# The last layer's S5 parameters in smaller pieces, over the merge and the output projection

## The chip, the cores and the metric

The kernel runs on one core of one Trainium2 chip. The core has five engines with a queue of instructions each: TensorE (PE in the profile, its weight loads PEld), VectorE (DVE), ScalarE (ACT), GpSimd (POOL) and SyncE (SP). Here SP starts most transfers, POOL starts the stores of the S5 parameters. The metric is the device time of one execution in microseconds (us).

## The reference

Two layers work on 512 latent and 256 context tokens of width 1024. In each layer an input projection feeds three branches (differential attention, RG-LRU, S5), each branch is gated and projected, the three are merged by sigmoid gates, and an output projection is added to the stream:

```python
def gated_merge(ya, yr, ys, za, zr, zs, gl, w_branch, w_out):
    y = jnp.stack([ya * jax.nn.silu(za), yr * jax.nn.silu(zr), ys * jax.nn.silu(zs)], axis=2)
    yb = jnp.einsum('btnw,nwd->btnd', y, w_branch)
    g = jax.nn.sigmoid(gl.reshape(*gl.shape[:2], N_BRANCH, D_MODEL))
    return jnp.sum(g * yb, axis=2) @ w_out
```

The S5 branch is a complex diagonal state space. Its coefficients depend on parameters alone:

```python
    mag = jnp.exp(lr * dt)
    ar = mag * jnp.cos(li * dt)
    ai = mag * jnp.sin(li * dt)
    ...
    br = cr[..., None] * b_re - ci[..., None] * b_im
    bi = cr[..., None] * b_im + ci[..., None] * b_re
```

So whatever the kernel derives from them for the second layer (powers of a, tables, products with B and C) can be computed at any time before that layer's scan.

## The kernel before

Weights are float32. `wsplit` (L159 to L161) loads a block `wr`, ACT rounds it to `wh`, DVE subtracts to get `wl`; the activations are split likewise (`hH`, `hL`). `product` (L174) sums three matmuls per block: `wh` with the high and low halves, `wl` with the high half. A product over 768 tokens with 8 blocks is 48 matmuls (a 512 and a 256 wide one each time).

The end of layer 0 goes like this. `merge_y` (four times) makes the gated attention output `yH`, `yL` from an input projection. `merge_g(0, ...)` then runs eight steps `dt`: a gate product `ps_in` (48 matmuls, two weight splits), a branch product `ps_b` (24, one split), `g` from both on DVE (L872) and its sum into `m` (L873, on POOL for the first two steps, on DVE after). Steps 0 to 5 are followed by an adaLN product (`ps_ada`, L130, then transposes `ps_adat`, L135, and a reduce `mods` on DVE, L137). Then the output projection takes eight products `acc` or `ps_w` from `mH`, `mL`, with a residual `xn` each (L1139); the last three do the context tokens first and their latent half in `second()`. The context norm (L196 to L209) reads the residuals.

Into this, layer 0 also puts the S5 parameters of layer 1, by a generator `prepare()` that is advanced with `prep(n)`: powers, then for each of 16 pairs `pa` (with coefficients and tables every fourth) `vv` (L453 to L455) and `wt` (L500 to L504) on DVE, a strip of small matmuls `ps_st5` (L467 to L472) copied by ACT to `strip`, and four transposes `ps_wt` (L511) copied by ACT to `ws`. All are stored to `s5d` and `s5td` in HBM by POOL and fetched by SP in layer 1. `PIECES` says how often the generator is advanced: in each of the four `merge_y`, in each step of `merge_g`, in each product of the output projection. With `(2, 2, 2, 2), (3,) * 8, (2,) * 8` the 22 pieces of before are used up in merge step 4.

The order on each engine is set by the tile layer's scheduler from the order of emission, the data, and the buffers that are free. Tables `tb`, `strip`, `wt` and `ws` have one buffer, `vv` and `Bb` two; strips, transposes, adaLN and norm share two PSUM buffers (`mis`).

Of the kernel before, what the change touches and what calls it, by code (L numbers as in the profile page):

```python
# [35 lines left out]
        [[0, 2], [1, 0], [2, 1], [1, 0], [0, 1, 1, 0], [0, 1, 1, 0, 3, 1, 1, 0]])  # L36
S5_BUFS = 3

PIECES = ((2, 2, 2, 2), (3,) * 8, (2,) * 8)
EARLY = {2: (1, 3, 4, 5, 6), 0: (1, 2, 3, 4, 5)}  # L40
LATE = 3
ADD_V = (2, 8)
# [9 lines left out]
def hybrid_kernel(ctx, tc, xT, cc, wmod, win, winv, wbr, wout, wglu, wlru, par, lqk, s5a, s5b, s5B, s5C, dsk, rope, outT):  # L52
# [311 lines left out]
    s5d = pD.tile([16, 128, R_N], F32, name="s5d")  # L364
    s5e = pD.tile([8, 128, 4, 128], F32, name="s5td")


    def s5_params(l, p, VV, E, store=None, storet=None):

# [3 lines left out]
        def cmul(eng, orr, oi, xr, xi, yr, yi, t1, t2):  # L373
            eng.tensor_mul(t1, xr, yr)
            eng.tensor_mul(t2, xi, yi)
            eng.tensor_sub(orr, t1, t2)
            eng.tensor_mul(t1, xr, yi)
            eng.tensor_mul(t2, xi, yr)
            eng.tensor_add(oi, t1, t2)

        def s5_powers():
            asc = [p.tile([128, 64, 9], F32, name=f"asc{c}", tag="vv", bufs=VV) for c in range(2)]
            V.memset(asc[0][:, :, 0:1], 1.0)
            V.memset(asc[1][:, :, 0:1], 0.0)
            V.tensor_copy(asc[0][:, :, 1:2], ar[:, l * 64:(l + 1) * 64].unsqueeze(2))
            V.tensor_copy(asc[1][:, :, 1:2], ai[:, l * 64:(l + 1) * 64].unsqueeze(2))
            ct = [p.tile([128, 64, 4], F32, name=f"ct{c}", tag="UW"[c]) for c in range(2)]
            for m in (1, 2, 4):
                sh = [128, 64, m]
                cmul(V, asc[0][:, :, m + 1:2 * m + 1], asc[1][:, :, m + 1:2 * m + 1], asc[0][:, :, 1:m + 1],  # L390
                     asc[1][:, :, 1:m + 1], asc[0][:, :, m:m + 1].to_broadcast(sh),
                     asc[1][:, :, m:m + 1].to_broadcast(sh), ct[0][:, :, :m], ct[1][:, :, :m])
            for c in range(2):
                w4 = pw[c].rearrange("p (r d g) n -> p r d g n", d=2, g=2)
                a4 = asc[c].rearrange("p (r d g) n -> p r d g n", d=2, g=2)
                for g2 in range(2):
                    V.memset(w4[:, :, 0, g2, 0:1], 0.0)
                    V.memset(w4[:, :, 1, g2, 9:10], 0.0)
                    V.tensor_copy(w4[:, :, 0, g2, 1:10], a4[:, :, 0, g2, :])
                    V.tensor_copy(w4[:, :, 1, g2, 8::-1], a4[:, :, 1, g2, :])  # L400

        def s5_coeffs(qt):

# [17 lines left out]
        def s5_tables(qt):  # L421

            tb = p.tile([128, 2, 8, NCH], F32, name="tb", tag="tb")
            tt = [p.tile([128, 2, 8, 24], F32, name=f"tt{c}", tag="UW"[c]) for c in range(2)]
            b0 = l * 32 + qt * 8
            V.memset(tb[:, 0, :, 0:1], 1.0)
            V.memset(tb[:, 1, :, 0:1], 0.0)
            V.tensor_copy(tb[:, 0, :, 1:2], f8r[:, b0:b0 + 8].unsqueeze(2))
            V.tensor_copy(tb[:, 1, :, 1:2], f8i[:, b0:b0 + 8].unsqueeze(2))
            m = 1  # L430
            while m < NCH - 1:
                c = min(m, 24, NCH - 1 - m)
                for e in range(2):
                    V.tensor_mul(tt[e][:, :, :, :c], tb[:, :, :, 1:1 + c],
                                 tb[:, e, :, m:m + 1].unsqueeze(1).to_broadcast([128, 2, 8, c]))
                V.tensor_sub(tb[:, 0, :, m + 1:m + 1 + c], tt[0][:, 0, :, :c], tt[1][:, 1, :, :c])
                V.tensor_add(tb[:, 1, :, m + 1:m + 1 + c], tt[0][:, 1, :, :c], tt[1][:, 0, :, :c])
                m += c
            tbs[qt] = tb
            if store is not None:  # L440
                for r in range(4):
                    G.dma_start(store[4 * qt + r, :, R_TB:].rearrange("p (e b j) -> p e b j", e=2, b=2),
                                tb[:, :, 2 * r:2 * r + 2, :])

        def s5_vv(pa):

            qt, pr = pa // 4, pa % 4
            qs, pq = slice(pr * 4, pr * 4 + 4), slice(pa * 4, pa * 4 + 4)
            xC = xCs[qt]
            vv = p.tile([128, 4, 10, 16], F32, name="vv", tag="vv", bufs=VV)  # L450
            vu = p.tile([128, 4, 10, 16], F32, name="vu", tag="wu")
            sh = [128, 4, 10, 16]
            E.tensor_mul(vv, xC[:, 0, qs].unsqueeze(2).to_broadcast(sh), pw[0][:, pq].unsqueeze(3).to_broadcast(sh))  # L453
            E.tensor_mul(vu, xC[:, 1, qs].unsqueeze(2).to_broadcast(sh), pw[1][:, pq].unsqueeze(3).to_broadcast(sh))
            E.tensor_sub(vv, vv, vu)  # L455
            vfs[pa] = vv.rearrange("p q n h -> p q (n h)")
            if store is not None:
                G.dma_start(store[pa, :, :R_WS].rearrange("p (q n) -> p q n", q=4), vfs[pa])
# [33 lines left out]
        def s5_wt(pa):  # L492
            qt, pr = pa // 4, pa % 4
            qs, pq = slice(pr * 4, pr * 4 + 4), slice(pa * 4, pa * 4 + 4)
            Bb = Bbs[qt]

            wt = p.tile([128, 4, 8, 16], F32, name="wt", tag="wt")
            wu = p.tile([128, 4, 8, 16], F32, name="wu", tag="wu")
            sh = [128, 4, 8, 16]
            E.tensor_mul(wt, Bb[:, 0, qs].unsqueeze(2).to_broadcast(sh),  # L500
                         pw[0][:, pq, 8:0:-1].unsqueeze(3).to_broadcast(sh))
            E.tensor_mul(wu, Bb[:, 1, qs].unsqueeze(2).to_broadcast(sh),
                         pw[1][:, pq, 8:0:-1].unsqueeze(3).to_broadcast(sh))
            E.tensor_add(wt, wt, wu)  # L504
            wts[pa] = wt

        def s5_ws(pa):
            wt = wts[pa]
            pwt = mis("ps_wt")
            for q in range(4):  # L510
                PE.transpose(pwt[:, q * 128:(q + 1) * 128], wt[:, q].rearrange("p s h -> p (s h)"), ident)  # L511
            ws = p.tile([128, 4, 128], F32, name="ws", tag="ws5")
            S.activation(ws.rearrange("p q n -> p (q n)"), pwt, AF.Copy)
            wss[pa] = ws
            if store is not None:
                G.dma_start(store[pa, :, R_WS:R_TB].rearrange("p (q n) -> p q n", q=4), ws)

        def prepare():

            s5_powers()  # L520
            yield
            for pa in range(16):
                if pa % 4 == 0:
                    s5_coeffs(pa // 4)
                    s5_tables(pa // 4)
                    yield
                s5_vv(pa)
                s5_wt(pa)
                yield
                s5_strip(pa)  # L530
                s5_ws(pa)

        return SimpleNamespace(powers=s5_powers, coeffs=s5_coeffs, tables=s5_tables, vv=s5_vv, strip=s5_strip,
# [3 lines left out]
    def s5_make(l):  # L537
# [7 lines left out]
        if l == 0:  # L545
            pr_ = s5_params(l, p5, S5_BUFS, V)
# [96 lines left out]
        def s5_inner(pa):  # L643
            if pa % 4 == 0:
                pr_.coeffs(pa // 4)
            pr_.vv(pa)
            pr_.strip(pa)

        def ahead():
            for st in sts:  # L650
                V.memset(st[:, :, :, 0:1], 0.0)
            if l > 0:
                for p in range(3):
                    fetch(p)
                return
            pr_.powers()
            s5_inner(0)
            done[0] = 1
            pr_.tables(0)

        def step(pa):
            if pa == 0:
                s5_input(0)
                s5_scan(0)
            if l == 0 and done[0] < 16:
                s5_inner(done[0])
                done[0] += 1
            if pa + 1 < 16:
                if pa % 4 == 3:
                    s5_input(pa // 4 + 1)  # L670
                    if l == 0:
                        pr_.tables(pa // 4 + 1)
                s5_scan(pa + 1)
            s5_out(pa)
            if l > 0:
                fetch(pa + 3)
# [5 lines left out]
    for l in range(L):  # L682
# [404 lines left out]
        if l == 0:  # L1087
            prst, pPr = pool("s5prep", 1, side="right")
            ast, pAd = pool("wmod2", 4, side="right")
            pieces = s5_params(1, pPr, 2, V, s5d, s5e).prepare()  # L1090

            def prep(n):
                for _ in range(n):
                    next(pieces, None)
# [6 lines left out]
        for i in range(4):  # L1101
            merge_y(ZA_T, oT, i, y0, 0.5)
            prep(PIECES[0][i])
        for dt in range(KT):
# [6 lines left out]
            elif dt in (1, 4):  # L1111
                adaln(1, 4 + dt // 4, pAd)
            prep(PIECES[1][dt])
        ast.close()
# [32 lines left out]
        for dt in range(KT):  # L1147
# [17 lines left out]
            residual(dt, po, sg)  # L1165
            prep(PIECES[2][dt])
        if need:
# [124 lines left out]
```

## Time and profile before

| | |
|---|---|
| median of 3 runs | 1634.73 us (1633.6 to 1636.02) |
| profiled execution | 1631.08 us, span 1629.3 us |
| TensorE matmul, weight load busy | 1503.6 us (92%), 1256.4 us (77%) |
| VectorE busy | 1170.3 us (72%) |
| ScalarE, POOL busy | 752.9 us (46%), 122.3 us (8%) |
| mean granted TensorE clock | 0.962 of full speed |

The profile is of one execution. Times on its axis are microseconds from the first instruction. A busy share is the time in which the engine has an instruction under way; starting a transfer and waiting are not counted as busy. The granted clock is the share of TensorE's full speed that it was allowed, 0.5 being 1.2 GHz and 1.0 being 2.4 GHz.

### The profile page before, as it was taken

How to read it: one execution, taken by the hardware profiler on the slowest of the kernel's cores; microseconds unless marked ns; L12 is line 12 of the kernel's file. 1: busy time of each engine (PE TensorE's matmuls, PEld its weight loads, DVE VectorE, ACT ScalarE, POOL GpSimd, SP SyncE). 2: the span in 40 equal slices, each digit the busy share in tenths (PEclk: the TensorE clock that was granted, in tenths of full speed). 3: DMA queues.
4: the chain of work that ended last, by engine and by line, in shares of the span. 5: the costliest groups of instructions: out<-in, count | busy, mean ns of one | idle time of the engine just before them, and what ended most of it. 6: DMA issues, size and time to landing. Idle time of an engine off the chain costs nothing. (4 is left out here: it accounts for less than half of the span.)

```text
span 1629.3 us, 24552 instructions
## 1 busy us (share of the span) xinstructions
PE 1503.6 (92%) x9096; PEld 1256.4 (77%) x9096; DVE 1170.3 (72%) x2463; ACT 752.9 (46%) x1300; POOL 122.3 (8%) x175
## 2 busy tenths in 40 slices
PE   4997569999999999996699999999899999999997
PEld 2776458888988888885577888777788888888877
DVE  7899999974457757759898445388877467488555
ACT  7674335542345434543233335576533355355433
POOL 1000000000000000001455000000000000000020
PEclk9999769999999999997799999999999999999999
DMA  8432112132211111113588550344445312212442
GB/s 286 154 103 64 52 50 67 53 109 78 59 58 39 46 52 46 46 33 128 185 261 281 184 179 33 122 143 140 119 149 145 103 59 69 62 59 65 140 168 94
DMA packets 103144, 174.43 MB, mean 107 GB/s; under 512 B 24432, under 2 KB 41456, under 8 KB 103024
## 3 DMA queue, kind: packets, MB, share of 16 engines
q1 hardware_dynamic: 97392, 158.17, 30.8%
q0 software_dynamic: 5632, 14.69, 2.8%
q8 instruction: 72, 1.18, 0.3%
q14 instruction: 48, 0.39, 0.1%
HBM read 145.02 MB, written 25.69 MB: 105 GB/s over the span
## 5 line engine op out<-in xcount | busy, mean ns | idle before, releaser
L160 ACT ACTIVATE wh<-wr 128x512 fp32r<-128x512 f32 x320 | 200.2, 630 | 403.4 <-PE ps_in L174 192.8
L174 PE MATMUL ps_in<-hH,wh 128*128 128x512 f32 x1248 | 375.3, 359 | 11.3 <-ACT m L828 4.8
L174 PE MATMUL ps_in<-hH,wl 128*128 128x512 f32 x1248 | 375.8, 358 | 8.8 <-DVE wl L161 8.8
L161 DVE TENSOR_TENSOR wl<-wr,wh 128x512 fp32r<-128x512 f32 x320 | 229.4, 720 | 208.4 <-ACT wh L160 162.1
L174 PE MATMUL ps_in<-hL,wh 128*128 128x512 f32 x1248 | 372.4, 357 | 0.0
L174 PEld LDWEIGHTS ps_in<-hH,wh 128*128 128x128 f32 x1248 | 205.9, 190 | 48.8 <-ACT m L828 5.6
L174 PEld LDWEIGHTS ps_in<-hH,wl 128*128 128x128 f32 x1248 | 207.1, 190 | 44.3 <-DVE wl L161 10.3
L174 PEld LDWEIGHTS ps_in<-hL,wh 128*128 128x128 f32 x1248 | 205.5, 190 | 31.6 <-issue 0.2
L873 POOL TENSOR_TENSOR m<-m,g 128x768 f32<-128x768 f32 (+1 forms) x16 | 28.2, 1764 | 1174.5 <-DVE g L872 749.3
L1038 ACT ACTIVATE p<-ps_s,mx 128x768 f32<-128x768 f32 (+1 forms) x80 | 65.2, 816 | 71.5 <-DVE mx L1037 67.6
L174 PE MATMUL ps_b<-yH,wh 128*128 128x512 f32 (+1 forms) x288 | 88.5, 358 | 1.8 <-ACT wh L160 1.8
L174 PE MATMUL ps_b<-yH,wl 128*128 128x512 f32 (+1 forms) x288 | 88.2, 358 | 0.2 <-DVE wl L161 0.2
L174 PE MATMUL ps_b<-yL,wh 128*128 128x512 f32 (+1 forms) x288 | 88.1, 358 | 0.0
L1036 DVE TENSOR_REDUCE mx<-ps_s 128x1 f32<-128x768 f32 (+1 forms) x80 | 67.6, 847 | 23.5 <-PE ps_s L1033 22.9
L174 PEld LDWEIGHTS ps_b<-yH,wh 128*128 128x128 f32 x288 | 47.9, 188 | 11.7 <-ACT wh L160 3.0
L174 PEld LDWEIGHTS ps_b<-yH,wl 128*128 128x128 f32 x288 | 47.7, 188 | 7.6 <-DVE wl L161 0.3
L174 PEld LDWEIGHTS ps_b<-yL,wh 128*128 128x128 f32 x288 | 47.6, 188 | 7.2
L174 PE MATMUL acc<-mH,wl 128*128 128x512 f32 (+1 forms) x160 | 49.0, 339 | 0.0
L511 PE MATMUL ps_wt<-ident,wt 128*128 128x128 f32 x128 | 24.0, 317 | 27.0 <-DVE wt L504 15.9
L174 PE MATMUL acc<-mH,wh 128*128 128x512 f32 (+1 forms) x160 | 48.7, 337 | 0.0
L174 PE MATMUL acc<-mL,wh 128*128 128x512 f32 (+1 forms) x160 | 48.7, 337 | 0.0
L1030 PE MATMUL ps_s<-ks,qs 128*128 128x256 f32 (+1 forms) x144 | 42.5, 367 | 3.3 <-ACT ks L1004 1.4
(349 smaller groups left out, 2843.1 us busy)
## 6 DMA issues: line engine op xcount, KB each, us to landing
wr<-in_win SPq DMA_DIRECT2D x208, 256.0 KB
wm<-in_wmod SPq DMA_DIRECT2D x48, 512.0 KB
wr<-in_wbr SPq DMA_DIRECT2D x48, 256.0 KB
sp<-s5d SPq DMA_DIRECT2D x16, 768.0 KB
wr<-in_wout SPq DMA_DIRECT2D x32, 256.0 KB
s5d<-vv POOLq DMA_DIRECT2D x16, 320.0 KB, 3.3
usd<-up SPq DMA_DIRECT2D x8, 512.0 KB
vt<-usd SPq DMA_DIRECT2D x64, 64.0 KB
```

What stands on the lines that cost most here:

```text
L160: S.activation(wh, raw, AF.Copy)
L161: V.tensor_sub(wl, raw, f32(wh))
L174: PE.matmul(out[:, c0:c0 + n], lhsT=(wl if ps == 2 else wh)[:, k, :], rhs=rhs(k0 + k, ps == 1)[:, t0:t0 + n], start=st, stop=en)
L511: PE.transpose(pwt[:, q * 128:(q + 1) * 128], wt[:, q].rearrange("p s h -> p (s h)"), ident)
L873: (V if n == 0 and dt >= ADD_V[l] else G).tensor_add(m_t[dt][:, :W], m_t[dt][:, :W], g[:, :W])
L1030: PE.matmul(sc[:, c0:c0 + w], lhsT=qs[:, c, qt * 128:(qt + 1) * 128], rhs=kk[:, c, t0:t0 + w], start=True, stop=False)
L1036: V.reduce_max(mx[:, 0:1], sc[:, :kw], axis=AX.X)
L1038: S.activation(p[c][:, :kw], sc[:, :kw], AF.Exp, bias=mx[:, 1:2], scale=0.125, accum_out=sm[:, c:c + 1])
```

## The change

The generator is cut finer and advanced differently. Powers are emitted in three pieces and not one, coefficients and tables in four and not one, and `vv` stands in a piece of its own, with strip and `wt` in the next. That makes 52 pieces of the 22. Of these four go into the four `merge_y`, 32 into the eight merge steps, and the other 16 into products 0 to 5 of the output projection. In layer 0's own use the same functions are run through with `whole`.

```diff
-PIECES = ((2, 2, 2, 2), (3,) * 8, (2,) * 8)
+PIECES = ((1, 1, 1, 1), (4,) * 8, (3, 3, 3, 3, 3, 2, 2, 2))
...
+    def whole(pieces):
+        for _ in pieces:
+            pass
...
                      asc[1][:, :, m:m + 1].to_broadcast(sh), ct[0][:, :, :m], ct[1][:, :, :m])
+                if m == 2:
+                    yield
+            yield
             for c in range(2):
...
                     V.tensor_copy(w4[:, :, 1, g2, 8::-1], a4[:, :, 1, g2, :])
+            yield
...
                 m += c
+                if m in (32, 80):
+                    yield
             tbs[qt] = tb
...
                                 tb[:, :, 2 * r:2 * r + 2, :])
+            yield
...
-            s5_powers()
-            yield
+            yield from s5_powers()
             for pa in range(16):
                 if pa % 4 == 0:
                     s5_coeffs(pa // 4)
-                    s5_tables(pa // 4)
                     yield
+                    yield from s5_tables(pa // 4)
                 s5_vv(pa)
+                yield
+                s5_strip(pa)
                 s5_wt(pa)
                 yield
-                s5_strip(pa)
                 s5_ws(pa)
...
-            pr_.powers()
+            whole(pr_.powers())
             s5_inner(0)
             done[0] = 1
-            pr_.tables(0)
+            whole(pr_.tables(0))
```

What it makes of the order is seen at three places. The first is VectorE at the weights of the merge's first gate (`wl_7737` before, `wl_7482` now). Before:

```order
L504 TENSOR_TENSOR wt_7729<-wt_7729,wu_7730 128x512
L434 TENSOR_TENSOR tt0_7681<-tb_7680 128x16x16
L434 TENSOR_TENSOR tt1_7682<-tb_7680 128x16x16
L161 TENSOR_TENSOR wl_7737<-wr_7735,wh_7736 128x512
L436 TENSOR_TENSOR tb_7680<-tt0_7681,tt1_7682 128x8x16
L437 TENSOR_TENSOR tb_7680<-tt0_7681,tt1_7682 128x8x16
L161 TENSOR_TENSOR wl_7743<-wr_7741,wh_7742 128x512
```

Now, with `sz`, `oT` and `yL` of the last `merge_y` beside it:

```order
L382 TENSOR_TENSOR bt1_7470<-xB_7461,cr_124 128x256
L846 SCALAR_TENSOR_TENSOR sz_7453<-sz_7453,ps_in_7404 128x768
L383 TENSOR_TENSOR Bb_7468<-bt0_7469,bt1_7470 128x256
L848 TENSOR_TENSOR oT_6614<-oT_6614,sz_7453 128x768
L161 TENSOR_TENSOR wl_7482<-wr_7480,wh_7481 128x512
L161 TENSOR_TENSOR wl_7488<-wr_7486,wh_7487 128x512
L161 TENSOR_TENSOR wl_7544<-wr_7542,wh_7543 128x512
L852 SCALAR_TENSOR_TENSOR yL_7458<-oT_6614,yH_7457 128x768
L434 MEMSET tb_7601 128x8
```

The split stood behind five pairs and a table and a half, 149 S5 and merge instructions in all with itself; now 51, and the first table comes after it. The second place is TensorE just before that gate (`ps_in_7747` before, `ps_in_7492` now). Before:

```order
L174 MATMUL ps_b_7803<-yL_7209,wh_7798 128x256
L467 MATMUL ps_st5_7395<-vv_7384,Bb_7261 16x128
L469 MATMUL ps_st5_7395<-vv_7384,Bb_7261 16x112
L467 MATMUL ps_st5_7395<-vv_7384,Bb_7261 16x128
L469 MATMUL ps_st5_7395<-vv_7384,Bb_7261 16x112
L472 MATMUL ps_st5_7395<-vv_7384,Bb_7261 16x16 x2
L511 MATMUL ps_wt_7407<-ident_105,wt_7390 128x128 x4
L467 MATMUL ps_st5_7495<-vv_7415,Bb_7261 16x128
L469 MATMUL ps_st5_7495<-vv_7415,Bb_7261 16x112
```

Now:

```order
L174 MATMUL ps_b_7548<-yL_7209,wh_7543 128x256
L130 MATMUL ps_ada_7575<-wm_7576,ccs_81 32x512 x2
L130 MATMUL ps_ada_7575<-wm_7580,ccs_81 32x512 x2
L130 MATMUL ps_ada_7575<-wm_7584,ccs_81 32x512 x2
L130 MATMUL ps_ada_7575<-wm_7588,ccs_81 32x512 x2
L135 MATMUL ps_adat_7594<-ident_105,stg_7592 128x128 x2
L174 MATMUL ps_in_7492<-hH_235,wl_7482 128x512
```

Before, the strips and transposes of five pairs stand ahead of the rest of the gate; now the first strip comes in merge step 2. The third place is VectorE in the output projection, around the residual of its first product (`xn_9254` before, `xn_8989` now). Before:

```order
L161 TENSOR_TENSOR wl_9316<-wr_9314,wh_9315 128x512
L1139 SCALAR_TENSOR_TENSOR xn_9254<-acc_9256,mods_115,xn_9254 128x512
L1139 SCALAR_TENSOR_TENSOR xn_9254<-acc_9256,mods_115,xn_9254 128x256
L161 TENSOR_TENSOR wl_9376<-wr_9374,wh_9375 128x512
L161 TENSOR_TENSOR wl_9382<-wr_9380,wh_9381 128x512
```

Now:

```order
L161 TENSOR_TENSOR wl_9101<-wr_9099,wh_9100 128x512
L465 TENSOR_TENSOR vu_9069<-xC_8604,pw1_7142 128x640
L1150 SCALAR_TENSOR_TENSOR xn_8989<-acc_8991,mods_115,xn_8989 128x512
L1150 SCALAR_TENSOR_TENSOR xn_8989<-acc_8991,mods_115,xn_8989 128x256
L466 TENSOR_TENSOR vv_9068<-vv_9068,vu_9069 128x640
L511 TENSOR_TENSOR wt_9094<-Bb_8610,pw0_7141 128x512
L513 TENSOR_TENSOR wu_9095<-Bb_8610,pw1_7142 128x512
L493 TENSOR_TENSOR strip_9050<-strip_9050,dskt_8607 16x4x16
L515 TENSOR_TENSOR wt_9094<-wt_9094,wu_9095 128x512
L161 TENSOR_TENSOR wl_9107<-wr_9105,wh_9106 128x512
```

S5 rows stand between the splits and the residuals, where there were none.

## Rows read from the trace of the kernel before

**Rows 1.** The page's 40 slices: busy tenths of TensorE, its granted clock.

```profile
PE   4997569999999999996699999999899999999997
PEclk9999769999999999997799999999999999999999
```

**Rows 2.** Stretches: length, then PE, PEld, DVE, ACT, POOL busy, clock, DMA, GB/s.

```profile
744.00:756.00 12.00, 10.17 (x58) 8.55 (x56) 12.00 (x59) 4.49 (x8) 0.33 (x1) 1.00 0.66 219
756.00:800.00 44.00, 20.71 (x130) 13.68 (x129) 43.79 (x113) 11.85 (x31) 17.76 (x33) 0.53 0.53 175
800.00:893.00 93.00, 88.54 (x635) 69.24 (x634) 82.48 (x182) 33.62 (x81) 53.31 (x90) 1.00 0.75 244
893.00:926.00 33.00, 33.00 (x195) 27.25 (x194) 15.23 (x22) 13.77 (x20) 2.50 (x7) 1.00 0.53 181
926.00:980.00 54.00, 54.00 (x328) 47.62 (x327) 25.07 (x45) 17.71 (x32) 0.00 (x0) 1.00 0.55 181
```

**Rows 3.** TensorE's waits, 740 to 920: us in all, times, longest.

```profile
PE ps_st L467 <- DVE vv L455: 12.1, 6, 5.6
PE ps_wt L511 <- DVE wt L504: 8.5, 4, 3.1
```

**Rows 4.** VectorE in order of time: start, us, instruction, idle before and releaser.

```profile
743.96 0.11 DVE L383 MEMSET asc<- 128x64 f32 x1
...
752.57 0.07 DVE L426 MEMSET tb<- 128x8 f32 x1
...
790.59 0.67 DVE L161 TENSOR_TENSOR wl<-wr,wh 128x512 fp32r<-128x512 f32 x1
...
807.27 0.95 DVE L872 SCALAR_TENSOR_TENSOR g<-g,ps_b 128x768 f32<-128x768 f32 x1 [4.20 <-PE ps_b L174]
...
897.32 0.95 DVE L872 SCALAR_TENSOR_TENSOR g<-g,ps_b 128x768 f32<-128x768 f32 x1 [0.29 <-PE ps_b L174]
...
912.56 0.96 DVE L872 SCALAR_TENSOR_TENSOR g<-g,ps_b 128x768 f32<-128x768 f32 x1 [3.31 <-PE ps_b L174]
...
925.28 0.95 DVE L872 SCALAR_TENSOR_TENSOR g<-g,ps_b 128x768 f32<-128x768 f32 x1 [2.93 <-PE ps_b L174]
...
976.24 0.48 DVE L1139 SCALAR_TENSOR_TENSOR xn<-acc,mods,xn 128x256 f32<-128x256 f32 x1 [1.04 <-PE acc L174]
```

**Rows 5.** TensorE in order of time, 755 to 826.

```profile
755.16 0.62 PE L174 MATMUL ps_b<-yH,wh 128*128 128x512 f32 x2 [1.83 <-ACT wh L160]
...
807.09 0.28 PE L467 MATMUL ps_st<-vv,Bb 128*16 128x128 f32 x1
...
807.47 0.66 PE L511 MATMUL ps_wt<-ident,wt 128*128 128x128 f32 x4
...
823.22 1.92 PE L130 MATMUL ps_ada<-wm,ccs 128*32 128x512 f32 x16
825.89 0.66 PE L135 MATMUL ps_adat<-ident,stg 128*128 128x128 f32 x4
```

**Rows 6.** A stretch of 10 us, columns as in rows 2.

```profile
820.00:830.00 10.00, 8.62 (x65) 5.74 (x65) 9.71 (x27) 4.74 (x14) 2.69 (x3) 1.00 0.77 259
```

**Rows 7.** VectorE by line and shape, 742 to 990: count, busy us, mean ns.

```profile
L453 DVE TENSOR_TENSOR vv<-xC,pw 128x640 f32<-128x640 f32 x16 | 13.0, 812 | 0.5 <-DMA s5d<-vv 0.5
...
L504 DVE TENSOR_TENSOR wt<-wt,wu 128x512 f32<-128x512 f32 x16 | 10.8, 678 | 0.0
```

**Rows 8.** POOL starting stores, and the issues by line with KB, us to landing.

```profile
770.79 2.89 POOL L442 DMA_DIRECT2D s5d<-tb  x4 [0.35 <-DVE tb L437]
...
781.93 4.06 POOL L485 DMA_DIRECT2D s5td<-strip  x8 [2.04 <-ACT xC L417]
...
s5d<-tb POOLq DMA_DIRECT2D x16, 192.0 KB, 2.9
```

**Rows 9.** ACT's waits, 800 to 920, as in rows 3.

```profile
ACT ws L513 <- DMA s5d<-ws: 8.6, 3, 5.1
```

**Rows 10.** The first S5 product of layer 1: ns min, median, max, first and last start.

```profile
L590 PE MATMUL ps_x<-vt,sp x176: 246/246/423, 1047.7 to 1177.2; 128*64 128x96 f32 x176
```

More of the change, by code (lines that the diff above doesn't have):

```diff
@@ L671, in step @@
                     if l == 0:
-                        pr_.tables(pa // 4 + 1)
+                        whole(pr_.tables(pa // 4 + 1))
                 s5_scan(pa + 1)
```

## The prediction

> **What bounds the kernel now.** I read the 40 slices of the page first. TensorE is at nine tenths or more nearly everywhere, but slices 19 and 20 (733 to 815 us) show 6 and 6, with 7 and 7 for the granted clock [rows 1]. The stretch is the end of layer 0's gated merge. Then I cut the neighbourhood into five stretches, from the first instruction of the S5 parameters to the context norm [rows 2]. From 744 to 800 VectorE is busy for 55.8 of 56 us; TensorE is busy for 10.17 of 12 us and then for 20.71 of 44 us at a granted clock of 0.53. From 800 to 893 both are nearly full (88.54 and 82.48 of 93 us). From 893 to 980 TensorE is full at clock 1.00 and VectorE is busy for 40.3 of 87 us. So one stretch is bound by VectorE, the next by both, the last by TensorE with VectorE half empty. The table of waits says what TensorE waited for: mostly the S5 products vv and wt on VectorE [rows 3]. Behind those TensorE's own matmuls are queued: the first split weight of the merge's first gate starts at 790.59 on VectorE, 46.6 us after the first S5 instruction at 743.96 [rows 4].
>
> What TensorE loses there: idle 1.8 us (744 to 756), 23.3 us (756 to 800), 4.5 us (800 to 893), together 29.6 us; and 20.71 us of work at clock 0.53 that would take 20.71 x 0.53 = 11.0 us at full clock, 9.7 us more. In all **39.3 us** [rows 2]. That is the most that feeding TensorE better can return in this stretch.
>
> **The change, part by part.** Nothing is computed less or more: 314 VectorE instructions of S5, 16 strip clusters and 16 transpose clusters on TensorE, 112 stores on POOL stand in both orders. They move.
>
> The front. By the order, 149 VectorE instructions stand between the first of S5 and the end of the first gate's split weight before, 51 now. Of the 51 rows 45 are S5, the powers and the first coefficients, which took 743.96 to 752.57, 8.6 us [rows 4]; five others (two sz, two oT, one yL) are as wide as g, 0.95 us each [rows 4], 4.7 us, and the last is the split itself: 13.3 us. So the gate's weights are split at about 757, 33 us earlier than 790.59. TensorE comes there at 755 to 758: it started the first branch product at 755.16 [rows 5], and now it has an adaLN product of 1.92 us to do before it needs wl. I count the front stall as gone, and with it the low clock. That short pauses leave the clock alone is seen at 820 to 830: 1.4 us idle in 10, clock 1.00 [rows 6].
>
> The merge steps. Before, the g of step 0 stands at 807.27 and that of step 5 at 897.32 [rows 4]: 18.0 us per step, with 4.46 us idle in them, so TensorE's own need is 17.1 us with 11 pairs' clusters in five steps. VectorE's need per step now: S5 is 134 us in all when each instruction counts at the mean of its form (the 96 instructions vv, vu, wt and wu make 71 us at 0.81 and 0.68 us, the tables most of the rest) [rows 7]. 11.7 us of it stand ahead of the first gate, 32.5 us behind the first output weights, so 90 us are left for eight steps, 11.2 each; with three splits at 0.72 and two adds at 0.95 us a step costs 15.3 us. In a full queue VectorE overlaps starts: the 58.3 us of means before the first split took 47.3 us, a factor of 0.81, so 12.4 us. It hides under TensorE's 17.1, with about 4 us to spare per step.
>
> The stores. The tables have one buffer and are stored by POOL: four stores took 2.89 us to issue and 2.9 us to land [rows 8], and in the new order the next table's first memset stands right behind the last add of the table before. I charge VectorE 5.8 us for each of three such turns, 17.4 us, against 8 x 4 = 32 us to spare: hidden. If that cover is gone, up to 17.4 us show.
>
> The output projection. Six pairs' vv, seven wt and one set of coefficients now stand between its weight splits: 32.5 us of means, on a stretch in which VectorE was busy for 25.07 of 54 us [rows 2]. 25.07 + 32.5 = 57.6 us on 54 + the S5 clusters' own TensorE time; by the factor 0.81 the 32.5 become 26, and 51 us fit. This is the tightest place: residuals and the context norm stand behind S5 rows there.
>
> What is left. TensorE still has to wait inside the S5 clusters: strip, its four ACT copies, transpose, one copy, in two PSUM buffers. In 800 to 893 the 11 clusters went with 4.46 us of idling, 0.41 us each [rows 2]. I take that for all 16: 6.6 us. Bounds: nothing, and the 39.3 us of now over 16, 2.5 us each. I take the nearest rows, in which VectorE was as full as it will be. Gain: 39.3 - 6.6 = **32.7 us**.
>
> Cross-check by steps. A step without S5 takes 12.7 us (925.28 less 912.56) for 72 matmuls, 0.177 us each [rows 4]. The g of step 0 comes after 757.3 + 44 and 20 matmuls (rest of gate, rest of branch, 7.8 + 3.5) + 1 = 769.6. Seven more steps are 88.9, five adaLN sums at 1.92 + 0.66 are 12.9, eight clusters at 1.04 (807.09 to 808.13) [rows 5] and 0.41 are 11.6: 113.4, so the last g is at 883.0 instead of 925.28, 42.3 us earlier. The eight clusters that now stand in the projection give back 11.6: **30.7 us**. I take 31 us, near the lower of the two, since it prices the clusters where they stand.
>
> After 980 the orders of TensorE are alike, so nothing is taken away again. The fetch of the first S5 sets for layer 1 now waits on SP for the last stores, near 940 by the times above; behind it on SP stand the last residual stores and the first LRU weights of layer 1. The sets' first reader stands at 1047.7 [rows 10], over 70 us later even when all moves up by 31: nothing.
>
> The profiled execution took 1631.08 us (span 1629.3), the median of the three runs is 1634.73, 0.2% more. The gain is taken from the median: 1634.7 - 31 = **1604 us**; its own range is a gain of 26 to 37, 1598 to 1609.
>
> **Rivals.**
> First, VectorE stays the bound. It has the same 179 us of work between 744 and 980, its instructions need not overlap, and it waits for stores. Everything up to the last residual at the mean of each form is 204 us (134 S5, 70 other); with the 17.4 us of table stores it ends at 744 + 204 + 17 = 965 instead of 976.7 [rows 4]: a gain of 11 us, 1624. For it: VectorE was over 99% busy in the bad stretch. Against: the factor 0.81, and that its work is now spread over 205 us.
>
> Second, all comes back: the clusters meet no wait since VectorE is ahead at each of them. 39.3 us, 1595. The same end is reached if TensorE has more to give in 800 to 893 than its idle time: its weight loads were busy for 69.24 us there, and from 926 to 980, where it never idled, for 47.62 of 54 us, a share of 0.88; 69.24/0.88 = 78.7 us would then be its need, 14.5 us free and not 4.5, the gain 31 + 10 = 41, the time 1594 [rows 2]. For it: leads of several us at steps 3 to 7. Against: two PSUM buffers, ACT copies between, and the five adaLN products, 5 x 1.92 = 9.6 us of long matmuls [rows 5], beside which a weight load is a small part of the time; so I keep the idle time, and both ways share a chance of 0.13. The count by weight loads is that of the Trainium skill, Perfetto Trace Analysis, section "Identifying the Most-Contended Engine": matmul busy time is no measure of what is left on TensorE, weight-load busy time is. The trace agrees where all matmuls are of one kind, and not where the adaLN products stand.
>
> Third, slower: ACT becomes the brake. ws and strip have one buffer; ACT waits for POOL's store of the last one before it copies, and the splits wh that TensorE needs stand behind that copy on ACT. Between 800 and 920 three such ws waits took 8.6 us, 2.9 each [rows 9], behind a VectorE that was late anyway. If all 16 turns showed on TensorE it would be 45.9 us, 6.6 more than can be won: 1641. It decides from 2.5 us per turn. Against: eight strip stores take 4.06 us to issue [rows 8] and a step takes 17.
>
> Fourth, no change: the waits move into the projection in full, since the context norm closes on residuals behind S5 rows. It would take 31 us there, 5 per product, with a VectorE that has 26 us of S5 in 60.
>
> **Chances.** Forecast 0.62, all back 0.13, VectorE-bound 0.17, slower 0.05, no change 0.03. The range from 1594 to 1619 holds the forecast, nearly all of the second and half of the first rival. 0.2% (3.3 us) is about what a measurement of this kernel can tell from no change: faster 0.92, same 0.03, slower 0.05.
>
> **What the profile after would show.** Right: the two 6s of TensorE and the dip of the clock are gone; the first gate's wl starts near 757; the last g of the merge near 884; VectorE is 70 to 90% busy up to 930; the context norm's last add about 30 us earlier than 977. Waits of TensorE for S5 under 10 us in all. Wrong: long waits of VectorE for table stores with TensorE idle behind them, ACT idle on stores with wh late, a clock under 1.00 in the projection, or residuals that come over 5 us behind their product.

## The result, and the profile after

The changed kernel took 1614.54 us in the median of four runs (1609.46 to 1617.99), the kernel before 1635.38 on the same chip: a ratio of 0.9872 (95% interval 0.9853 to 0.9891), 20.8 us faster. Timed a second time, it took 1610.51 us against 1633.79, ratio 0.9869 (0.9850 to 0.9888), 23.3 us. The forecast was 1604 in a range of 1594 to 1619: the direction, the range and the place were right, the gain was two thirds to three quarters of the 31 us. 1614.5 lies outside the forecast's own 1598 to 1609, midway between 1604 and the first rival's 1624; the range holds it because it was made to hold half of that rival. The profiled execution took 1609.46 us, the lowest of the four; its span is 1607.6 us.

The slices of the page, as [rows 1]:

```profile
PE   4997569999999999999898999899899999999997
...
PEclk9999779999999999999999999999999999999999
```

The two 6s and the two 7s of the clock are gone; slices 20 and 22 (764 to 804 and 844 to 884 us) show an 8 of TensorE instead. The stretches of [rows 2], same columns (length, PE, PEld, DVE, ACT, POOL busy, clock, DMA, GB/s):

```profile
744.00:756.00 12.00, 12.00 (x74) 10.63 (x73) 11.98 (x46) 4.21 (x8) 0.00 (x0) 1.00 0.59 198
756.00:800.00 44.00, 38.61 (x242) 30.12 (x241) 36.44 (x96) 12.09 (x24) 18.38 (x18) 0.96 0.59 198
800.00:893.00 93.00, 87.97 (x571) 70.07 (x570) 81.20 (x186) 33.77 (x67) 34.97 (x65) 0.96 0.63 205
893.00:926.00 33.00, 32.73 (x238) 27.73 (x237) 27.32 (x47) 13.31 (x34) 11.98 (x23) 1.00 0.77 261
926.00:980.00 54.00, 51.27 (x340) 44.70 (x340) 39.46 (x78) 29.53 (x67) 11.94 (x23) 1.00 0.59 200
```

The same sum as before the change, idle time of TensorE plus what the low clock costs: idle 0 + 5.4 + 5.0 + 0.3 + 2.7 = 13.4 us, clock 0.04 x 38.61 + 0.04 x 87.97 = 5.1 us, together 18.5 where it was 39.3. The difference, 20.8 us, is the measured gain. So the account holds; by the forecast 8 us of it should have been left, and 18 are. Where they are, TensorE's waits from 740 to 980 say (us in all, times, longest):

```profile
PE ps_wt L522 <- DVE mods L137: 9.1, 2, 4.6
PE ps_st L478 <- ACT strip L491: 2.8, 4, 2.0
```

The waits for vv and wt of [rows 3] are gone. A new pair stands in their place, for `mods`, the adaLN reduce on VectorE that frees a shared PSUM buffer. VectorE, as [rows 4]:

```profile
759.12 1.88 DVE L161 TENSOR_TENSOR wl<-wr,wh 128x512 fp32r<-128x512 f32 x3
...
771.99 0.95 DVE L883 SCALAR_TENSOR_TENSOR g<-g,ps_b 128x768 f32<-128x768 f32 x1
...
781.66 0.69 DVE L161 TENSOR_TENSOR wl<-wr,wh 128x512 fp32r<-128x512 f32 x1
787.88 0.07 DVE L434 MEMSET tb<- 128x8 f32 x1 [5.54 <-DMA s5d<-tb]
787.90 0.17 DVE L436 COPY tb<-f8r 128x8 f32<-128x8 f32 x1
787.91 0.07 DVE L435 MEMSET tb<- 128x8 f32 x1
788.01 0.95 DVE L883 SCALAR_TENSOR_TENSOR g<-g,ps_b 128x768 f32<-128x768 f32 x1
...
792.82 0.18 DVE L137 TENSOR_REDUCE mods<-ps_adat 128x8 f32<-128x32 f32 x1
...
848.44 0.07 DVE L434 MEMSET tb<- 128x8 f32 x1 [5.05 <-DMA s5d<-tb]
...
895.21 0.95 DVE L883 SCALAR_TENSOR_TENSOR g<-g,ps_b 128x768 f32<-128x768 f32 x1 [2.17 <-PE ps_b L174]
...
974.66 0.75 DVE L1150 SCALAR_TENSOR_TENSOR xn<-acc,mods,xn 128x512 f32<-128x512 f32 x1
```

Read it from the top. The first gate's split starts at 759.12 (before 790.59; forecast 757) and the g of step 0 at 771.99 (forecast 769.6): the front came as worked out, 2.4 us late. Then VectorE stands 5.54 us at the first memset of table 1, because the one table buffer is still being stored; the g of step 1 and, a dozen instructions on, the reduce `mods` stand behind it. At 848.44 the same happens again, with the first memset of table 3. The last g comes at 895.21, not at 883.0. On TensorE, the two stalls (idle before the instruction, and releaser, in brackets):

```profile
793.06 0.92 PE L522 MATMUL ps_wt<-ident,wt 128*128 128x128 f32 x4 [4.64 <-DVE mods L137]
...
849.40 1.11 PE L522 MATMUL ps_wt<-ident,wt 128*128 128x128 f32 x4 [4.49 <-DVE mods L137]
```

And TensorE's clock behind them, which is not under 1.00 in the stretch right ahead of the first:

```profile
788.00:793.00 5.00, 0.42 (x1) 0.11 (x1) 4.83 (x16) 1.05 (x4) 2.10 (x1) 1.00 0.96 332
793.00:797.00 4.00, 3.94 (x24) 3.27 (x25) 3.79 (x10) 1.65 (x5) 1.23 (x3) 0.57 0.55 214
797.00:800.00 3.00, 3.00 (x20) 2.64 (x19) 2.11 (x5) 1.23 (x2) 3.00 (x7) 1.00 0.31 53
...
850.00:853.00 3.00, 3.00 (x21) 2.45 (x20) 2.44 (x6) 1.65 (x5) 1.73 (x4) 0.50 0.49 188
```

After 4.6 us without work the next 4 us run mostly at 1.2 GHz (0.57), then at 2.4 again; behind the second stall 3 us run at 1.2 GHz (0.50).

The output projection went as priced: its eight clusters make the way from the last g to the last residual 974.66 - 895.21 = 79.5 us, where it was 993.54 - 925.28 = 68.3; 11.2 us, and the forecast said 11.6. Before, the last residual was this one:

```profile
993.54 0.74 DVE L1139 SCALAR_TENSOR_TENSOR xn<-acc,mods,xn 128x512 f32<-128x512 f32 x1
```

### The profile page after: what moved, and what is told of

Same layout as the page of the kernel before. It is cut to its first block, busy times and chain, and to the rows that moved or that the text cites. A ratio compares the mean times of both kernels' runs of the same rounds, so it can differ in the third digit from the quotient of the medians.

```text
span 1607.6 us, 24547 instructions
## 1 busy us (share of the span) xinstructions
PE 1496.6 (93%) x9096; PEld 1253.3 (78%) x9096; DVE 1171.6 (73%) x2463; ACT 751.9 (47%) x1300; POOL 126.0 (8%) x175
## 5 line engine op out<-in xcount | busy, mean ns | idle before, releaser
L884 POOL TENSOR_TENSOR m<-m,g 128x768 f32<-128x768 f32 (+1 forms) x16 | 34.2, 2135 | 1104.1 <-DVE rc L1052 426.1
L174 PE MATMUL ps_g<-uHL,wh 128*128 128x512 f32 (+1 forms) x128 | 34.5, 384 | 11.5 <-ACT uHL L803 7.3
```

The lines of the kernel that those rows point to most:

```text
L174: PE.matmul(out[:, c0:c0 + n], lhsT=(wl if ps == 2 else wh)[:, k, :], rhs=rhs(k0 + k, ps == 1)[:, t0:t0 + n], start=st, stop=en)
L884: (V if n == 0 and dt >= ADD_V[l] else G).tensor_add(m_t[dt][:, :W], m_t[dt][:, :W], g[:, :W])
```

## The experiments

Each was timed beside the kernel before. "Lost" is the account of above for 744 to 980, over the same five stretches of that kernel, idle plus clock; "by it" is 39.3 less that.

| kernel | us, median | ratio to before (95%) | faster by | lost: idle + clock | by it |
|---|---|---|---|---|---|
| the change | 1614.54 | 0.9872 (0.9853 to 0.9891) | 20.8 | 13.4 + 5.1 | 20.8 |
| the change again (e9) | 1610.51 | 0.9869 (0.9850 to 0.9888) | 23.3 | 15.2 + 4.9 | 19.2 |
| two tables (e1) | 1611.99 | 0.9865 (0.9845 to 0.9885) | 21.5 | 12.8 + 4.7 | 21.8 |
| three tables (e7) | 1612.09 | 0.9876 (0.9858 to 0.9894) | 21.7 | 15.0 + 6.1 | 18.2 |
| pinned tables (e6) | 1614.84 | 0.9885 (0.9867 to 0.9904) | 19.0 | 17.4 + 8.1 | 13.8 |
| pinned, other amounts (e13) | 1614.87 | 0.9892 (0.9874 to 0.9910) | 17.2 | 16.2 + 6.3 | 16.8 |
| tables between pairs (e12) | 1607.30 | 0.9838 (0.9817 to 0.9860) | 26.0 | 9.8 + 0 | 29.5 |
| one table only (e8) | 1605.57 | 0.9827 (0.9807 to 0.9846) | 28.2 | 10.4 + 1.8 | 27.1 |
| two strips (e11) | 1610.97 | 0.9860 (0.9836 to 0.9884) | 22.4 | 13.3 + 6.4 | 19.6 |
| spread only (e2) | 1627.91 | 0.9970 (0.9958 to 0.9982) | 5.6 | 24.2 + 11.4 | 3.7 |
| split only (e3) | 1646.44 | 1.0091 (1.0075 to 1.0106) | -12.9 | 37.7 + 16.2 | -14.6 |
| before, two tables (e5) | 1642.63 | 1.0065 (1.0051 to 1.0080) | -9.1 | 35.7 + 14.3 | -10.7 |
| tables on POOL (e10) | 1646.90 | 1.0079 (1.0061 to 1.0098) | -13.6 | 44.8 + 14.6 | -20.1 |

The last column follows the measured gain to about 5 us (6.5 in the last row), where the gains range over 42: most of what these kernels differ in is TensorE's idle time in this stretch and the clock behind it. One profiled execution is set against a median, and single profiles of the same kernel differ too (e9 and the change).

**Spread only (e2).** The kernel before, its coarse pieces spread.

```diff
-PIECES = ((2, 2, 2, 2), (3,) * 8, (2,) * 8)
+PIECES = ((1, 1, 1, 1), (1, 1, 1, 1, 2, 1, 2, 1), (1,) * 8)
```

> The kernel before with its 22 coarse pieces, but spread as in the change: 4 in merge_y, 10 in the merge, 8 in the output projection. Theory A (the amount ahead of a weight split matters, not the grain): the stall ahead of the first gate is nearly gone, 1612 to 1621. Theory B (the grain matters: coefficients, a whole table or three products and the strip in one piece hold VectorE for 5 to 10 us each): four tables stall TensorE for 4 us or more each, 1623 to 1634.

1627.91 us: theory B. TensorE, two of its stalls:

```profile
773.22 0.27 PE L467 MATMUL ps_st<-vv,Bb 128*16 128x128 f32 x1 [4.11 <-DVE vv L455]
...
811.03 1.10 PE L511 MATMUL ps_wt<-ident,wt 128*128 128x128 f32 x4 [4.55 <-DVE mods L137]
```

The front is better than before (31.33 us of TensorE in 756 to 800, clock 0.84, where it was 20.71 and 0.53), but seven stalls of 2.0 to 4.6 us are left up to 914 us, most of them for vv, wt or `mods`.

**Split only (e3).** The changed kernel, advanced as far as before at each place.

```diff
-PIECES = ((1, 1, 1, 1), (4,) * 8, (3, 3, 3, 3, 3, 2, 2, 2))
+PIECES = ((6, 5, 5, 5), (6, 8, 8, 6, 3, 0, 0, 0), (0,) * 8)
```

> The changed kernel with its fine pieces, but advanced as far as in the kernel before at each place: 21 in merge_y, then 6, 8, 8, 6, 3 in merge steps 0 to 4, none after. Theory A (the amount): VectorE again has about 46 us of S5 ahead of the first gate's split, and the time is that of the kernel before, 1630 to 1638. Theory B (the grain): the scheduler can put the splits between fine pieces, 1615 to 1624.

1646.44 us, slower than before, which neither theory had, though A was nearer. The front is nearly as bad as before:

```profile
756.00:800.00 44.00, 22.11 (x149) 15.92 (x150) 43.74 (x113) 13.05 (x34) 16.62 (x30) 0.65 0.43 138
```

From 744 to 800 it loses 29.7 us by the account, 5 less than before. The rest comes later: in 800 to 893 TensorE idles 15.7 us at a clock of 0.89, where before it idled 4.5 at 1.00; 6.3 us of that are three waits for wt, vv and wt between 872 and 880. So neither half of the change is worth much by itself: spreading alone 5.6 us, splitting alone less than nothing, both 21 to 23.

**Two tables (e1).** The first theory for the missing 10 us: the wait for the table's store.

```diff
-            tb = p.tile([128, 2, 8, NCH], F32, name="tb", tag="tb")
+            tb = p.tile([128, 2, 8, NCH], F32, name="tb", tag="tb", bufs=2 if store is not None else 1)
```

> The changed kernel with two buffers for the tables tb and not one. Theory A (table turn): the changed kernel misses the forecast because VectorE, in order, stood 5.54 and 5.05 us at the first memset of a new table until POOL's stores of the last one had landed, with the adaLN reduce that frees a PSUM buffer behind it; TensorE lost 4.64 + 4.49 us and ran some 7 us at half clock after it (about 3 us more). Then both waits go and the time is 1614.5 - 12 = 1602 (1600 to 1606), with no TensorE idle over 2.5 us between 756 and 930. Theory B (VectorE's S5 work itself is the brake, the wait only shows where its debt is paid): waits for vv or wt take their place, 1611 to 1616. Theory C (the two shared PSUM buffers): half of each stall stays, 1607 to 1610.

1611.99 us, not told apart from the changed kernel: theory A fails, though one wait for a store is left. VectorE and TensorE at the place of the first stall:

```profile
777.50 0.07 DVE L434 MEMSET tb<- 128x8 f32 x1
...
788.73 0.07 DVE L434 MEMSET tb<- 128x8 f32 x1 [3.50 <-DMA s5d<-tb]
```

```profile
793.76 1.12 PE L522 MATMUL ps_wt<-ident,wt 128*128 128x128 f32 x4 [7.12 <-DVE mods L137]
```

With a second buffer free, the scheduler's order pulls table 1 forward to 777.50 and has VectorE stand for table 2 at 788.73, in the same step; the stall of TensorE at this place grew from 4.64 to 7.12 us, the other shrank from 4.49 to 2.21.

**Before with two tables (e5).** The same edit in the kernel before.

> The kernel before with two buffers for tb. Theory A (table turn, a wait that the change brought): before it had one wait of VectorE for a table's store, 0.41 us; 1633 to 1637, no change. Theory B (VectorE's work is what counts, or the turn cost time before too): 1624 to 1631.

1642.63 us: both theories are wrong, it is 9.1 us slower. Two tables now start 3.4 us apart, two steps of pairs follow without a gap, and the next gate's split stands behind them until 854.93 (VectorE, then TensorE):

```profile
818.11 0.07 DVE L426 MEMSET tb<- 128x8 f32 x1
...
821.55 0.07 DVE L426 MEMSET tb<- 128x8 f32 x1
...
854.93 0.68 DVE L161 TENSOR_TENSOR wl<-wr,wh 128x512 fp32r<-128x512 f32 x1
```

```profile
855.66 1.01 PE L174 MATMUL ps_in<-hH,wl 128*128 128x512 f32 x2 [4.40 <-DVE wl L161]
```

So a free buffer alone, with nothing computed more, can move table work ahead of a gate and cost time.

**Pinned tables (e6), three tables (e7), one table (e8), the change again (e9).** Pinned: the seeds of tables 1 to 3 take a zero multiple of the vv ahead of them, so no order can begin them earlier.

```diff
+                pin = vfs[4 * qt - 1][:, 0, 0:8].unsqueeze(2)
+                V.tensor_scalar(tb[:, 0, :, 0:1], pin, 0.0, 1.0, op0=OP.mult, op1=OP.add)
...
+                V.scalar_tensor_tensor(tb[:, 0, :, 1:2], pin, 0.0, f8r[:, b0:b0 + 8].unsqueeze(2), op0=OP.mult, op1=OP.add)
...
```

> The changed kernel, one table buffer, but tables 1 to 3 are begun from a zero multiple of the vv product ahead of them, so that VectorE's order can't take them earlier than they were emitted: the first memset of table 1 then stands some 19 instructions behind the last add of table 0, and not next to it. Theory P (place: wherever a table buffer is free in the plan, the next table is pulled forward, and VectorE does or waits for a table while the gate's splits and the adaLN reduce stand behind it): no stall over 2.5 us from 760 to 930, 1601 to 1606. Theory W (the wait for the store alone): the same, since the store has landed, 1601 to 1606. Theory V (VectorE has too much S5 work in the merge wherever it stands): 1610 to 1616.

> The changed kernel with three table buffers. Two gave 1612, with a wait of VectorE of 3.50 us for a third table and a TensorE stall of 7.1 us at step 1. With three no table waits for a store any more. Theory W: the stalls go, 1601 to 1606. Theory P: three tables in a row now stand ahead of step 1's reduce and splits, some 12 us of VectorE each, and the stall at step 1 is 7 us or more: 1609 to 1620. Theory V: 1610 to 1616.

For one table the generator yields where tables 1 to 3 would stand, and table 0's store is issued 16 times.

> The changed kernel with tables 1 to 3 left out (table 0 is stored 16 times in their place, all at once). It takes some 3 x 12 us of VectorE out of the merge and the projection, and all turns of the table buffer. Theory V: with VectorE relieved TensorE never waits for it, and the time falls below the pinned kernel's by over 5 us: 1592 to 1600. Theories P and W: the pinned kernel has already lost these stalls, so it is within 4 us of it: 1600 to 1606.

> The changed kernel itself, unchanged, run beside the three others so that they are compared on one chip: 1610 to 1618, all theories.

Pinned took 1614.84 us, three tables 1612.09, one table 1605.57, and the change, timed beside them, 1610.51. Pinning took every wait of VectorE for a table's store away, and the time did not fall: the times of theories P and W fail. The merge did get shorter. The stretch with the first stall is nearly full, and the last g comes 5.7 us earlier than in the changed kernel:

```profile
756.00:800.00 44.00, 43.03 (x280) 34.78 (x272) 34.32 (x76) 12.51 (x25) 20.13 (x21) 1.00 0.62 210
```

```profile
889.48 0.95 DVE L890 SCALAR_TENSOR_TENSOR g<-g,ps_b 128x768 f32<-128x768 f32 x1 [0.70 <-PE ps_b L174]
```

But the projection then held table 3 and took 979.50 - 889.48 = 90.0 us instead of 79.5, with a stall of TensorE for the strip, which ACT copied late because the store of the last strip had not landed:

```profile
907.51 0.28 PE L485 MATMUL ps_st<-vv,Bb 128*16 128x128 f32 x1 [3.86 <-ACT strip L498]
```

```profile
906.37 0.27 ACT L497 ACTIVATE strip<-ps_st 16x128 f32<-16x128 f32 x1 [3.80 <-DMA s5td<-strip]
```

So pinning does not show that the waits for table stores cost nothing. The merge gained 5.7 us, without them and with a table less, and the projection lost 10.5; what the waits alone cost is not told apart.

Three buffers gave 7.28 us of stall at step 1, as theory P had it; one wait for a store was left even there (3.92 us), since all four tables had been pulled forward to 789.96. Only leaving out tables gave what theory V asked for, and not all of it: 5 us less than the change, where V had 1592 to 1600.

**Tables between pairs (e12), and the pinned kernel with its amounts (e13).** What was left: the amount of VectorE work, or its standing in a row. In e12 each table starts from the vv of its first pair and its three pieces stand behind the first three pairs of its set; 36 pieces and not 32 are advanced in the merge steps. Table 3, which the changed kernel's order had pulled into the merge, is held back here.

```diff
-PIECES = ((1, 1, 1, 1), (4,) * 8, (3, 3, 3, 3, 3, 2, 2, 2))
+PIECES = ((1, 1, 1, 1), (5, 5, 5, 5, 4, 4, 4, 4), (2, 2, 2, 2, 2, 2, 0, 0))
...
-                    yield from s5_tables(pa // 4)
+                    tab = s5_tables(pa // 4)
...
                 s5_ws(pa)
+                if pa % 4 < 3:
+                    next(tab, None)
+                    yield
```

> The pinned kernel with the three pieces of a table set between its pairs (one after each of the first three) and not in a row ahead of them, and advanced by 5, 5, 5, 5, 4, 4, 4, 4 in the merge and six times 2 in the projection. Pinning alone gave 1614.8: no wait for a table's store, a merge 6 us shorter than in the changed kernel and a projection 10 us longer, with a table of 44 instructions in it. Theory S (what stalls TensorE is a run of VectorE instructions in a row, a table above all): even pieces leave stalls under 2 us and give 1602 to 1608. Theory V (VectorE's amount): nothing is computed less, 1610 to 1617.

1607.30 us: theory S. Every instruction of S5 is still there. Its stretches:

```profile
756.00:800.00 44.00, 41.96 (x281) 33.25 (x280) 39.47 (x88) 14.14 (x30) 15.64 (x23) 1.00 0.65 220
800.00:893.00 93.00, 89.17 (x606) 68.98 (x605) 78.44 (x175) 37.24 (x79) 45.36 (x68) 1.00 0.61 207
...
926.00:980.00 54.00, 50.05 (x334) 44.33 (x332) 37.34 (x76) 32.20 (x66) 10.26 (x19) 1.00 0.58 189
```

VectorE is as busy as in the changed kernel (199.1 against 196.4 us in 744 to 980), but no stall of TensorE is over 2 us before 978 and the clock stays at 1.00. (Of the idling in the last row 1.7 us belong to a wait for `hH` that the slower kernels have after 980.) The control has the same amounts with each table in a row (the first not pinned):

> The pinned kernel, each table in a row as there, but advanced by 5, 5, 5, 5, 4, 4, 4, 4 in the merge and six times 2 in the projection, as in the kernel with the tables between the pairs (1607.3); pinned with the change's own amounts took 1614.8. Theory S (a run of table instructions in a row is what stalls TensorE): the amounts alone give little, 1611 to 1616. Theory A (the amounts in the projection decide): 1604 to 1609.

1614.87 us, ratio 0.9892 (0.9874 to 0.9910) against 0.9838 (0.9817 to 0.9860): the amounts alone give nothing, the place of the pieces gives 8 to 9 us (7.6 by the medians, 8.8 by the gains). TensorE's two longest stalls there:

```profile
800.73 0.81 PE L529 MATMUL ps_wt<-ident,wt 128*128 128x128 f32 x4 [4.13 <-DVE wt L522]
...
904.80 1.01 PE L174 MATMUL acc<-mH,wl 128*128 128x512 f32 x2 [4.39 <-DVE wl L161]
```

Theory S says that a run of table instructions stalls TensorE, and these two stalls do not show that. Ahead of the first VectorE was idle: `wt` stood behind a split that waited for ACT, and ACT waited for the store of the last `ws` (ACT, then VectorE):

```profile
798.14 0.60 ACT L531 ACTIVATE ws<-ps_wt 128x512 f32<-128x512 f32 x1 [6.76 <-DMA s5d<-ws]
```

```profile
799.28 0.69 DVE L161 TENSOR_TENSOR wl<-wr,wh 128x512 fp32r<-128x512 f32 x1 [4.33 <-ACT wh L160]
```

Ahead of the second stand the low halves `mL` and a set of coefficients; the next table begins at 905.61. The third (2.79 us, at 851.00, for `mods`) does have half a table ahead of it. ACT's wait alone does not make the difference either: in e12 ACT waits 7.14 us for a `ws` store until 798.86, and TensorE's longest stall near it is 1.30 us. So it is shown that the place of the pieces matters, and that what stalls TensorE is an instruction that it needs standing on VectorE behind something slow, be it work or a wait. That a table in a row is that something in these two kernels is not shown.

e12 is the fastest complete version, by 3 to 5 us of gain over the changed kernel (26.0 against 23.3 and 20.8); the intervals of their ratios to before overlap by 0.0010 at most.

**Two strips (e11).** `strip` and `ws` with two buffers each (`bufs=2` in their two lines).

> The changed kernel with two buffers each for strip and ws. ACT waited 7.2 us in three turns for stores of ws; TensorE waited 2.8 us for strip copies, which stand behind ACT's other work. Theory A (these waits are off the path): 1609 to 1615, as the changed kernel. Theory B (the third rival of the prediction, ACT as the brake): 1600 to 1607.

1610.97 us, as the change: theory A. These waits are off the path here. The same edit was not tried on e6 or e13, where waits for these stores stand behind a stall.

**Tables on POOL (e10).** Tables 1 to 3 issued to POOL (`Q = G if store is not None and qt else V` in place of `V` through the function).

> The changed kernel with tables 1 to 3 computed by POOL and not by VectorE. Leaving these tables out gave 1605.6. Theory V (VectorE's amount of work beside the gates decides): VectorE gets the same relief, 1603 to 1609. Theory K (POOL and VectorE slow each other, and POOL's stores queue behind its tables): one add of POOL as wide as a g took 2.10 us where VectorE took 0.95, so a table of 12 us on VectorE takes some 26 us on POOL, 80 us in all beside 78 us that it has; vv and ws are then stored late, VectorE waits for their buffers, and the time is that of the changed kernel or more, 1611 to 1622.

1646.90 us, far beyond what either had. POOL, ACT and TensorE at the worst place:

```profile
882.56 2.93 POOL L453 DMA_DIRECT2D s5d<-tb  x4 [0.30 <-POOL tb L446]
...
886.33 0.61 POOL L528 DMA_DIRECT2D s5d<-ws  x1
```

```profile
888.84 0.60 ACT L525 ACTIVATE ws<-ps_wt 128x512 f32<-128x512 f32 x1 [29.61 <-DMA s5d<-ws]
```

```profile
891.22 1.01 PE L174 MATMUL ps_in<-hH,wh 128*128 128x512 f32 x2 [19.18 <-ACT g L840]
```

The store of a `ws` stands on POOL behind a whole table; ACT waits 29.61 us for its buffer, with the weights' roundings and the gate's sigmoid behind it. This is the third rival of the prediction, under a condition that it did not name: a long queue on POOL.

## Why the prediction was right, and where its size was off

- **The front stall** would go, with its clock: right. Split at 759.12 (757), first g at 771.99 (769.6), nothing idle in 744 to 756.
- **What it would return** (39.3 us at most): the account held in size, to 6.5 us, for all kernels of the table.
- **The cover in the merge**, "It hides under TensorE's 17.1, with about 4 us to spare per step", and for the table stores "17.4 us, against 8 x 4 = 32 us to spare: hidden": this is the step that failed. Spare time added up over eight steps says nothing on the order within one. VectorE works in order, and what TensorE needs (a split, a g, a reduce) stood behind a wait of 5.54 and then of 5.05 us for a table's store and the table work after it. Two stalls of 4.64 and 4.49 us and 5.1 us of low clock behind them are 14.2 us that had been put at nothing; with the start late by 2.4 us, and 2.5 us less of idling at the eight clusters of the merge (0.8 us of strip waits where 8 x 0.41 = 3.3 had been put down), that comes to 14.1 us; the last g missed 883.0 by 12.2. The term that failed is the one called hidden.
- **The size of the cover** was too large as well. From the first g to the last VectorE was busy for 102.4 us in seven steps, 14.6 each and not 12.4, and unevenly (10.3 to 18.8 us per step); seven `mL` of 0.95 us each, which the sum left out, are part of it.
- **The stores**, "If that cover is gone, up to 17.4 us show": 10.6 us of VectorE's waits showed, in two of the three turns. The sign of being wrong that was named for it, long waits of VectorE for table stores with TensorE idle behind them, was there. What the waits cost in the end is open. Without them, and without table 3, the merge was 5.7 us shorter in e6; in e13, with four more pieces in the merge, the last g came at 896.44, no earlier. With two or three buffers other table work took the wait's room.
- **The projection**, "the tightest place": 11.2 us for eight clusters, priced 11.6. Right; in e6, with a table more and fewer clusters, it took 10.5 us more. The context norm's last add, forecast some 30 us earlier than 977, moved from 977.21 to 958.51, 18.7 us, near the measured gain.
- **First rival** (VectorE-bound, 1624): its mechanism is half of the truth, since e8 gained with less VectorE work; but e12 had the same work and nearly the same time as e8, so amount alone is not the bound. **Second** (all back, 1595, or more by the count of weight loads, 1594): not seen in any kernel; e8 and e12 keep 9.8 to 10.4 us of idling. **Third** (ACT behind stores): not in this kernel (e11), but real (e10, and one stall each of e6 and e13). **Fourth**: excluded by the intervals.

What stays open: which part of the missing 10 us the waits for table stores are and which the table work; whether e12 gains on e13 by breaking up the tables or by keeping needed instructions out from behind ACT's waits; which of the remaining 10 us of e12 can be had; and why the part of the span behind the last residual differs by up to 6 us between single profiles (635.8 before, 632.9 and 631.0 in two of the changed kernel, 637.0 in e6).

## What to carry to other kernels

Where filler work shares an in-order engine with work that another engine waits for, look at the longest stretch of filler, its waits included, between two of the waited-for instructions, not at its mean per step. Here splitting and spreading paid only together, and the scheduler undid some of the spreading where data and buffers allowed: a real dependence held a piece in its place (e6, e12), a second buffer set it loose (e1, e5). Before a change is costed, add idle time and clock loss of the bound engine over the stretch: the sum says what can be won, and after it where the rest is.

## What the runs showed of the hardware that was not expected

An add on POOL and single instructions of VectorE were slower beside each other. In the changed kernel, POOL's sums of step 0 and step 1, and VectorE's copy of one shape beside the second sum and later (spans on POOL are rough):

```profile
773.10 7.54 POOL L884 TENSOR_TENSOR m<-m,g 128x768 f32<-128x768 f32 x1 [7.38 <-DVE mods L137]
...
789.12 2.10 POOL L884 TENSOR_TENSOR m<-m,g 128x768 f32<-128x768 f32 x1 [4.21 <-DVE g L883]
```

```profile
789.48 1.77 DVE L437 COPY tb<-f8i 128x8 f32<-128x8 f32 x1
...
848.54 0.17 DVE L437 COPY tb<-f8i 128x8 f32<-128x8 f32 x1
```

The same add took 7.54 us amid table work on VectorE (as long in e1, e6 and e8), and 1.8 to 2.3 us at the other places, before, in e12 and in e13; a copy of 8 columns took 1.77 us beside it and 0.17 us alone. The Trainium skill, "SBUF — State Buffer", section "Who interferes with whom", calls the pair of ports that the two engines share an exclusive lock, with the one that issues first holding it for its whole instruction. The first copy agrees, since it ended at 791.25 and the add at 791.22; no run here takes it apart from other causes.

The landing of a table's store was longer than the median of 2.9 us before [rows 8]: issued by POOL from 839.71 to 842.67, its buffer came free at 848.44, 5.8 us later, with the DMA engines busy for 0.97 of 845 to 850.
